# Sliding windows on one core: mixing stores of 4 KB runs and of 8 KB runs throughout

## Chip, cores and metric

One core of a Trainium2 chip. The metric is device time of one execution in microseconds (us); a median of several runs is given. Before: 196.94 us.

## The reference

The input is 16 images of 64 channels, 64 x 64, float32 (16.8 MB). Every 8 x 8 window at stride 4 is copied out, 15 x 15 windows per image (59.0 MB). There is no arithmetic.

```python
for i in range(n_h):
    for j in range(n_w):
        result[:, i, j] = x[:, :, 4*i : 4*i + 8, 4*j : 4*j + 8]
```

## The kernel before

The whole input is loaded into `L`. A partition holds an image, half of the channels (`ch`) and a quarter of the rows. `window(j, s, half)` builds on DVE (the vector engine), in the ring buffer `G`, the windows of column `j` and row slot `s` of all partitions, and GpSimd (POOL) issues one indirect store. A store of all 32 channels of a partition writes 128 runs of 8 KB; one of half of them writes 128 runs of 4 KB. In the last slot one partition in four has no window, and its index is out of bounds.

```python
UNITS = 18                                   # ring of 18 half-size buffers
G = gpool.tile([P, UNITS * HCL, WS, WS], f32, name="G")

def window(j, s, half):                      # half: 0, 1, or None for all channels
    ...                                      # next buffer g in the ring
    if not last:
        nc.vector.tensor_copy(out=g, in_=L[:, cs, s * ST : s * ST + WS, cols])
    else:                                    # lower rows come from the next partition
        nc.vector.tensor_copy(out=g[:, :, 0:ST, :], in_=L[:, cs, s * ST : RB, cols])
        nc.vector.stream_shuffle(out=g[:, :, ST:WS, :], in_=L[:, cs, 0:ST, cols], mask=nxt)
    ...
    st = nc.gpsimd.indirect_dma_start(out=o, out_offset=..., in_=g..., ...)

order = [(j, s) for j in range(NW) for s in range(NSLOT)]   # 60 windows
EARLY = 12
for half in range(2):
    for j, s in order[:EARLY]:
        window(j, s, half)                   # 24 stores of 4 KB runs
for j, s in order[EARLY:]:
    window(j, s, None)                       # 48 stores of 8 KB runs
```

The first halves of the early windows need only half of the loads, so they go out while the rest is loaded. After that the kernel is a stream of stores.

Of the kernel before, what the change touches and what calls it, by code (L numbers as in the profile page):

```python
# [1 line left out]

# [4 lines left out]


@with_exitstack  # L10
def kernel(
    ctx: ExitStack,
    tc: tile.TileContext,
    x: bass.AP,
    window_size: int,
    stride: int,
    out: bass.AP,
):
    nc = tc.nc
    P = nc.NUM_PARTITIONS  # L20

    B, C, H, W = x.shape
    Bo, NH, NW, Co, WSo, WSo2 = out.shape
    WS = int(window_size)
    ST = int(stride)
    assert Bo == B and Co == C and WSo == WS and WSo2 == WS

    f32 = mybir.dt.float32
    i32 = mybir.dt.int32
    ALU = mybir.AluOpType  # L30
    HQ = 4
    CH = P // (B * HQ)
    CL = C // CH
    RB = H // HQ
    NSLOT = RB // ST
    NWIN = NH * NW
    CFREE = CL * WS * WS
    assert HQ == 4 and CH == 2 and WS == 2 * ST

    lpool = ctx.enter_context(tc.tile_pool(name="lpool", bufs=1))  # L40
    ipool = ctx.enter_context(tc.tile_pool(name="ipool", bufs=1))
    gpool = ctx.enter_context(tc.tile_pool(name="gpool", bufs=1))


    L = lpool.tile([P, CL, RB, W], f32)
    x_v = x.rearrange("b (ch cl) (hq r) w -> hq (b ch) cl (r w)", ch=CH, hq=HQ)
    NCH = 4
    cw = CL // NCH
    for k in range(NCH):
        for q in range(HQ):  # L50
            (nc.sync, nc.scalar)[q % 2].dma_start(
                out=L[q::HQ, k * cw : (k + 1) * cw, :, :],
                in_=x_v[q, :, k * cw : (k + 1) * cw, :],
            )


    def itile(name):
        return ipool.tile([P, 1], i32, name=name)

    pi, tb, tq, tc_, idx, idx_last = (itile(n) for n in ("pi", "tb", "tq", "tc", "idx", "idx_last"))  # L60
    nc.gpsimd.iota(pi[:, :], pattern=[[0, 1]], base=0, channel_multiplier=1)  # L61
    nc.vector.tensor_scalar(out=tb[:, :], in0=pi[:, :], scalar1=3, scalar2=None, op0=ALU.logical_shift_right)  # L62
    nc.vector.tensor_scalar(out=tc_[:, :], in0=pi[:, :], scalar1=2, scalar2=1, op0=ALU.logical_shift_right, op1=ALU.bitwise_and)  # L63
    nc.vector.tensor_scalar(out=tq[:, :], in0=pi[:, :], scalar1=HQ - 1, scalar2=None, op0=ALU.bitwise_and)  # L64
    nc.vector.tensor_scalar(out=tb[:, :], in0=tb[:, :], scalar1=float(NWIN * CH), scalar2=None, op0=ALU.mult)  # L65
    nc.vector.tensor_tensor(out=tb[:, :], in0=tb[:, :], in1=tc_[:, :], op=ALU.add)  # L66
    nc.vector.tensor_scalar(out=tc_[:, :], in0=tq[:, :], scalar1=float(NSLOT * NW * CH), scalar2=None, op0=ALU.mult)  # L67
    nc.vector.tensor_tensor(out=idx[:, :], in0=tb[:, :], in1=tc_[:, :], op=ALU.add)  # L68

    nc.vector.tensor_scalar(out=tq[:, :], in0=tq[:, :], scalar1=float(HQ - 1), scalar2=float(2 * B * NWIN * CH), op0=ALU.is_equal, op1=ALU.mult)  # L70
    nc.vector.tensor_tensor(out=idx_last[:, :], in0=idx[:, :], in1=tq[:, :], op=ALU.add)  # L71


    HCL = CL // 2
    idx_h, idx_hlast = itile("idx_h"), itile("idx_hlast")
    for d, e in ((idx_h, idx), (idx_hlast, idx_last)):
        nc.vector.tensor_scalar(out=d[:, :], in0=e[:, :], scalar1=2.0, scalar2=None, op0=ALU.mult)  # L77
    o_v = out.rearrange("b i j (ch cl) r w -> (b i j ch) (cl r w)", ch=CH)
    o_h = out.rearrange("b i j (ch cl) r w -> (b i j ch) (cl r w)", ch=2 * CH)
    nxt = [min(p + 1, 31) for p in range(32)]  # L80


    UNITS = 18
    G = gpool.tile([P, UNITS * HCL, WS, WS], f32, name="G")
    at = 0

    def window(j, s, half):
        nonlocal at
        cols = slice(j * ST, j * ST + WS)
        last = s == NSLOT - 1  # L90
        if half is None:
            n, c0 = 2, 0
            at += at % 2
        else:
            n, c0 = 1, half * HCL
        u = at % UNITS
        at += n
        cs = slice(c0, c0 + n * HCL)
        g = G[:, u * HCL : (u + n) * HCL, :, :]
        if not last:  # L100
            nc.vector.tensor_copy(out=g, in_=L[:, cs, s * ST : s * ST + WS, cols])  # L101
        else:
            nc.vector.tensor_copy(out=g[:, :, 0:ST, :], in_=L[:, cs, s * ST : RB, cols])  # L103
            nc.vector.stream_shuffle(out=g[:, :, ST:WS, :], in_=L[:, cs, 0:ST, cols], mask=nxt)  # L104
        if half is None:
            o, ix = o_v, (idx_last if last else idx)
        else:
            o, ix = o_h, (idx_hlast if last else idx_h)
        st = nc.gpsimd.indirect_dma_start(  # L109
            out=o,  # L110
            out_offset=bass.IndirectOffsetOnAxis(ap=ix[:, 0:1], axis=0),
            in_=g.rearrange("p c r w -> p (c r w)"),
            in_offset=None,
            element_offset=(s * NW + j) * CH * CFREE + (half or 0) * HCL * WS * WS,
            bounds_check=B * NWIN * CH * (1 if half is None else 2) - 1,
            oob_is_err=False,
        )
        tc.declare_no_dep(st.ins, group="stores", reason="each store writes rows of its own")
        tc.add_to_no_dep_group("stores", st.ins)

    order = [(j, s) for j in range(NW) for s in range(NSLOT)]
    EARLY = 12
    for half in range(2):
        for j, s in order[:EARLY]:
            window(j, s, half)
    for j, s in order[EARLY:]:
        window(j, s, None)


# [1 line left out]
_INS = ['x', 'window_size', 'stride']  # L131
_OUTS = [((16, 15, 15, 64, 8, 8), 'float32')]

_NUMBERS = {'window_size': 8, 'stride': 4}


# [26 lines left out]
```

## Time and profile before

| | before |
|---|---|
| time, profiled span | 196.94 us, 194.9 us |
| DVE, POOL busy | 85.7 us (44%), 91.1 us (47%) |
| DMA: packets, bytes, mean | 14,723; 75.8 MB; 389 GB/s |
| stores | 72 |

Read this as a transfer problem. The DMA row of the page is at 9 nearly everywhere, and both engines are half idle.

### The profile page before, as it was taken

How to read it: one execution, taken by the hardware profiler on the slowest of the kernel's cores; microseconds unless marked ns; L12 is line 12 of the kernel's file. 1: busy time of each engine (PE TensorE's matmuls, PEld its weight loads, DVE VectorE, ACT ScalarE, POOL GpSimd, SP SyncE). 2: the span in 40 equal slices, each digit the busy share in tenths (PEclk: the TensorE clock that was granted, in tenths of full speed). 3: DMA queues.
4: the chain of work that ended last, by engine and by line, in shares of the span. 5: the costliest groups of instructions: out<-in, count | busy, mean ns of one | idle time of the engine just before them, and what ended most of it. 6: DMA issues, size and time to landing. Idle time of an engine off the chain costs nothing.

```text
span 194.9 us, 458 instructions
## 1 busy us (share of the span) xinstructions
DVE 85.7 (44%) x119; POOL 91.1 (47%) x77
## 2 busy tenths in 40 slices
DVE  2000069100699865464646464747474737430000
POOL 0000037723388888888854545454545454530000
DMA  5999999999999889999999999999999999999970
GB/s 182 419 401 415 409 409 414 423 420 419 419 415 421 353 334 387 403 414 398 403 409 405 414 405 407 410 403 412 407 414 407 412 409 409 409 407 419 422 298 20
DMA packets 14723, 75.79 MB, mean 389 GB/s; under 512 B 1984, under 2 KB 1984, under 8 KB 8960
## 3 DMA queue, kind: packets, MB, share of 16 engines
q0 software_dynamic: 10368, 58.99, 74.7%
q1 hardware_dynamic: 2176, 8.39, 10.9%
q10 hardware_dynamic: 2176, 8.39, 10.6%
q14 instruction: 3, 0.02, 0.0%
HBM read 16.78 MB, written 62.91 MB: 409 GB/s over the span
## 4 chain that ended last, share of the span: by engine, by line
DMA 52%; issue 28%; POOL 8%; POOLq 1%; PEldq 0%
DMA out_dram<-G,idx_last 38%; DMA out_dram<-G,idx_hlast 15%; POOL out_dram L109 8%; POOLq L158 1%; POOLq L109 0%; POOL pi L61 0%; PEldq L158 0%
## 5 line engine op out<-in xcount | busy, mean ns | idle before, releaser
L101 DVE COPY G<-L 128x2048 f32<-128x2048 f32 (+1 forms) x54 | 55.8, 1055 | 69.5 <-DMA L<-in_x_dram 39.5
L109 POOL DMA_INDIRECT out_dram<-G,idx x36 | 44.8, 1244 | 31.8 <-DMA out_dram<-G,idx 27.4
L109 POOL DMA_INDIRECT out_dram<-G,idx_h x18 | 22.5, 1250 | 37.8 <-DVE G L101 28.8
L109 POOL DMA_INDIRECT out_dram<-G,idx_last x12 | 16.7, 1392 | 8.9 <-DVE G L104 7.7
L104 DVE STREAM_SHUFFLE G<-L 128x1024 f32<-128x1024 f32 (+1 forms) x18 | 19.6, 1088 | 0.0
L103 DVE COPY G<-L 128x1024 f32<-128x1024 f32 (+1 forms) x18 | 11.6, 643 | 16.0 <-DMA out_dram<-G,idx 14.4
L109 POOL DMA_INDIRECT out_dram<-G,idx_hlast x6 | 6.8, 1130 | 3.7 <-DMA out_dram<-G,idx_hlast 2.5
L62 DVE TENSOR_SCALAR tb<-pi 128x1 int32<-128x1 int32 x1 | 0.2, 154 | 1.0 <-POOL pi L61 1.0
L61 POOL IOTA pi<- 128x1 int32 x1 | 0.1, 119 | 0.4 <-PEq L158 0.4
L104 DVE LOAD_MASK_SELECT G<-L x18 | 0.2, 12 | 0.0
L144 POOL MEMSET const-float32-0.0<- 128x1 f32 x1 | 0.1, 98 | 0.2 <-issue 0.2
L68 DVE CUSTOM_DVE_ANT_0 idx<-tb,tc 128x2 uint16<-128x2 uint16 x1 | 0.2, 160 | 0.0
L66 DVE CUSTOM_DVE_ANT_0 tb<-tb,tc 128x2 uint16<-128x2 uint16 x1 | 0.2, 159 | 0.0
L67 DVE TENSOR_SCALAR tc<-tq 128x1 int32<-128x1 int32 x1 | 0.2, 154 | 0.0
L77 DVE TENSOR_SCALAR idx_hlast<-idx_last 128x1 int32<-128x1 int32 x1 | 0.2, 154 | 0.0
L77 DVE TENSOR_SCALAR idx_h<-idx 128x1 int32<-128x1 int32 x1 | 0.2, 154 | 0.0
L71 DVE CUSTOM_DVE_ANT_0 idx_last<-idx,tq 128x2 uint16<-128x2 uint16 x1 | 0.2, 153 | 0.0
L65 DVE TENSOR_SCALAR tb<-tb 128x1 int32<-128x1 int32 x1 | 0.1, 149 | 0.0
L70 DVE TENSOR_SCALAR tq<-tq 128x1 int32<-128x1 int32 x1 | 0.1, 148 | 0.0
L63 DVE TENSOR_SCALAR tc<-pi 128x1 int32<-128x1 int32 x1 | 0.1, 145 | 0.0
L64 DVE TENSOR_SCALAR tq<-pi 128x1 int32<-128x1 int32 x1 | 0.1, 144 | 0.0
L144 POOL MEMSET const-uint8-127<- 128x1 uint8 x1 | 0.1, 118 | 0.0
(2 smaller groups left out, 0.2 us busy)
## 6 DMA issues: line engine op xcount, KB each, us to landing
L<-in_x_dram SPq DMA_DIRECT2D x8, 1024.0 KB, 19.9
L<-in_x_dram ACTq DMA_DIRECT2D x8, 1024.0 KB, 21.3
out_dram<-G,idx POOLq DMA_INDIRECT x36, 18.7
out_dram<-G,idx_h POOLq DMA_INDIRECT x18, 8.7
out_dram<-G,idx_last POOLq DMA_INDIRECT x12, 18.5
out_dram<-G,idx_hlast POOLq DMA_INDIRECT x6, 8.9
```

The costliest lines, as they stand in the source:

```text
L62: nc.vector.tensor_scalar(out=tb[:, :], in0=pi[:, :], scalar1=3, scalar2=None, op0=ALU.logical_shift_right)
L66: nc.vector.tensor_tensor(out=tb[:, :], in0=tb[:, :], in1=tc_[:, :], op=ALU.add)
L67: nc.vector.tensor_scalar(out=tc_[:, :], in0=tq[:, :], scalar1=float(NSLOT * NW * CH), scalar2=None, op0=ALU.mult)
L68: nc.vector.tensor_tensor(out=idx[:, :], in0=tb[:, :], in1=tc_[:, :], op=ALU.add)
L71: nc.vector.tensor_tensor(out=idx_last[:, :], in0=idx[:, :], in1=tq[:, :], op=ALU.add)
L77: nc.vector.tensor_scalar(out=d[:, :], in0=e[:, :], scalar1=2.0, scalar2=None, op0=ALU.mult)
L101: nc.vector.tensor_copy(out=g, in_=L[:, cs, s * ST : s * ST + WS, cols])
L103: nc.vector.tensor_copy(out=g[:, :, 0:ST, :], in_=L[:, cs, s * ST : RB, cols])
L104: nc.vector.stream_shuffle(out=g[:, :, ST:WS, :], in_=L[:, cs, 0:ST, cols], mask=nxt)
L109: st = nc.gpsimd.indirect_dma_start(out=o, out_offset=bass.IndirectOffsetOnAxis(ap=ix[:, 0:1], axis=0), in_=g.rearrange("p c r w -> p (c r ...
L144: nc = _bacc.Bacc("TRN2", target_bir_lowering=False, num_devices=1)
L158: with _tile.TileContext(nc) as tc:
```

## The change

The intent is to alternate short and long stores: the short ones drain faster than POOL issues them, and the long ones give it time. In the mixed part the second halves of the early windows alternate with full stores; afterwards one window in three is split in halves, so that the mixture goes on to the end.

```diff
-    for half in range(2):
-        for j, s in order[:EARLY]:
-            window(j, s, half)
-    for j, s in order[EARLY:]:
-        window(j, s, None)
+    for j, s in order[:EARLY]:
+        window(j, s, 0)
+    late = list(order[:EARLY])
+    rest = list(order[EARLY:])
+    while late:
+        for w in late[:2]:
+            window(*w, 1)
+        for w in rest[:2]:
+            window(*w, None)
+        late, rest = late[2:], rest[2:]
+    while rest:
+        window(*rest[0], 0)
+        window(*rest[0], 1)
+        for w in rest[1:3]:
+            window(*w, None)
+        rest = rest[3:]
```

There are 84 stores for 72. Twelve full stores became 24 half stores.

## The prediction

> **What bounds the kernel now.** I began with the page's busy strip. DVE (44% of the span) and POOL (47%) are half idle, and the DMA row is at 9 from the second slice to the 38th. The kernel moves 16.8 MB in and 59.0 MB out, so the question is how fast the sixteen DMA engines drain, and where they do not. I asked for the stages separately (columns: stretch, its length, DVE and POOL busy us with instruction counts, clock, DMA share, GB/s):
>
> ```profile
> 51.00:66.00 15.00, 15.00 (x26) 12.02 (x9) 1.00 1.03 418
> 66.00:73.00 7.00, 4.28 (x5) 5.78 (x5) 1.00 0.78 315
> 73.00:101.00 28.00, 15.04 (x15) 22.41 (x18) 1.00 1.00 403
> 101.00:171.00 70.00, 39.63 (x43) 36.22 (x29) 1.00 1.01 408
> 171.00:188.00 17.00, 1.28 (x3) 1.92 (x2) 1.00 0.99 407
> 188.00:195.00 7.00, 0.00 (x0) 0.00 (x0) 1.00 0.18 77
> ```
>
> The DMA engines are full from 51 to 66 us, where the second halves of the first twelve windows go out as 4 KB runs. They are short of work in one place, 66 to 73 us (0.78), and slightly below full while the 8 KB stores run. The last row is the drain of the slower engines and the closing sequence.
>
> Why 66 to 73 starves is in the timeline (start, length, engine, what, and in brackets the idle time before it):
>
> ```profile
> 59.30 3.48 DVE L101 COPY G<-L 128x2048 f32<-128x2048 f32 x3
> 60.93 1.97 POOL L109 DMA_INDIRECT out_dram<-G,idx_h  x1 [0.30 <-issue]
> ...
> 63.20 1.01 POOL L109 DMA_INDIRECT out_dram<-G,idx_hlast  x1 [0.30 <-DMA out_dram<-G,idx_hlast]
> ...
> 64.48 2.41 DVE L101 COPY G<-L 128x2048 f32<-128x2048 f32 x2
> 64.52 2.50 POOL L109 DMA_INDIRECT out_dram<-G,idx_h  x1 [0.30 <-DMA out_dram<-G,idx_h]
> 67.32 0.96 POOL L109 DMA_INDIRECT out_dram<-G,idx_h  x1 [0.31 <-issue]
> ```
>
> What to see: each POOL instruction issues one store. During DVE copies it lasts 1.97 or 2.50 us; alone it lasts 0.96. The twelve half stores after 51 us start at 51.54 to 70.48, one per 1.72 us (18.94/11), but a half store drains in about 1.27 us (below). POOL loses 0.45 us per store, uses up the backlog left from the loads, and at 67 us the engines run dry.
>
> Then POOL's waits (total us, times, longest) and the DMA issues (last number: median us from issue to landing):
>
> ```profile
> POOL out_dram L109 <- DMA out_dram<-G,idx: 27.7, 24, 1.6
> out_dram<-G,idx POOLq DMA_INDIRECT x36, 18.7
> out_dram<-G,idx_h POOLq DMA_INDIRECT x18, 8.7
> ```
>
> An 8 KB store lands 18.7 us after its issue, about 7 stores of work at one per 2.44 us (four windows, one with 96 rows, per 9.77 us). The landing records use eight semaphores in turn, so POOL waits for the store eight back: the queue is limited to eight stores, whatever their size. In the late stage it is always deep; DVE and POOL only have to keep it from emptying.
>
> Finally I read the single landings and packets in the trace. Each store gives 16 landings, one per DMA engine, in two groups of eight. For the store landing at about 77 us the first and last engine are 0.16 us apart, at 161 us 3.4 us, at the end 3.5 us. So eight slower engines set the end: they take about 2.60 us per 8 KB store, the others 2.50. During 4 KB stores the spread stays at 0.8 to 1.0 us and does not grow. Packet times agree: 4 KB is 159 ns nearly always; 8 KB is 309 at best and 322 on average (338 while POOL issues beside a shuffle, 315 when neither works). The last data land at 191.2; closing takes 3.7 us, and the measured time is 2.0 above the span.
>
> **What the Trainium skill says.** "DMA: Bandwidth & Descriptors", section "Where 436 GB/s comes from", puts the ceiling of 16 engines at 435 GB/s. By that, 4 KB on one engine is 151 ns and 8 KB 301 ns (my estimate from the page); the trace's minima, 159 and 309, are each 8 ns more, so they agree with a ceiling and a small cost per packet. The same page, "Why small descriptors are slow (HBM only)", says that each packet has a fixed overhead of about 3 cycles; the trace shows such an overhead, about 8 ns. "SBUF — State Buffer", section "SBUF: two separate sides", says that DVE's fp32 SBUF-to-SBUF copy locks GpSimd out while it runs, so that it can't write DMA descriptors. The trace agrees: the POOL instruction of 2.50 us lies beside 2.41 us of copies.
>
> **The change part by part.** The first twelve half stores and their loads stay as they are; nothing moves before 51 us. Of the following, 12 of 48 full windows become 24 half windows (9 complete pairs and 3 last-slot pairs), interleaved with the twelve second halves so that two halves alternate with two fulls to the end. There are 84 stores for 72.
>
> 1. *The dip, removed.* On the slow engines, the landings from 68.0 to 76.9 us cover three halves, one last half and one full: 3×1.28 + 0.97 + 2.55 = 7.36 us of work in 8.9, so 1.5 us were idle, and another 0.1 at the next store: 1.6 us. After the change POOL issues 3 MB per four stores, which drains in 2×1.27 + 2×2.55 = 7.6 us; at its bad pace of 1.72 us POOL needs 6.9. The backlog at 51 us is seven half stores, to 58.7 us, so the first full stores are behind work already queued. DVE can fill about 11 free half-size buffers and then waits for landings, which also releases POOL. I see no dip: −1.6 us.
>
> 2. *More packets, added.* Splitting an 8 KB run costs 2×159 − 309 = 9 ns, for eight runs per engine 72 ns, plus one 9 ns completion packet: 0.08 us per full window. The last-slot windows count as 0.75, so 11.25 × 0.08 = +0.9 us over undisturbed 8 KB packets.
>
> 3. *Slow packets, moved.* On the slow engines a full store takes 2.60, not 2.48 (8×309 + 9 ns), and two halves 2.56. If 4 KB packets are really immune, those windows get shorter: 11.25 × (2.56 − 2.60) = −0.45, in place of +0.9. If instead the loss belongs to each POOL issue (about 0.09 us, 3.4 us over 38 stores), the 12 extra issues meet 8 KB packets two thirds of the time, and the full stores lose more: the +0.9 stays and up to +0.3 joins it. I take the middle, +0.4.
>
> 4. *Instructions.* Twelve copies of 1.24 us turn into 24 of about 0.67: +1.2 us on DVE (shuffles similar: 0.71 for half of 1.28). POOL has 12 more issues of 1.0 to 1.4 us: about +15. Both lie beside the DMA; DVE has idle gaps of 1.4 us at every late wait. Path: 0.
>
> Sum: −1.6 + 0.4 = −1.2, so 196.9 becomes 195.7 us.
>
> **Rivals.** *The shallower queue starves.* Eight mixed stores are 6 MB, not 8. At 2.5 us per MB that is 15 us. Fast engines 3.5 us ahead still have over 8 us queued when the eighth store back lands, and a new issue takes under 2 us. I don't expect it; if the alternation made POOL late anyway, I would see DMA share near 0.95 and 199 to 203 us. *POOL becomes the bound.* 84 issues with 1.7 to 2.5 us beside copies: if the mean were over 1.9 us per store, as in 59 to 67 us now, the dip would spread over the mixed stage. Against it: copies take only half of DVE's time once buffers are full (issues then last 0.96 to 1.39 now). It would give 198 to 201. *The dip is hidden anyway:* the fast engines wait 2.3 us there and the slow ones catch up by the difference, so the spread starts again at 0.16. Without the dip the existing 0.9 us spread is kept and grows. I counted slow engines alone for this reason; if they have some slack I missed, the gain is nil and steps 2 and 3 leave 197 to 198. *Best case:* immunity of the 4 KB packets holds, −2.05: 194.9.
>
> **Range and chances.** The certain parts are the dip (0 to −1.6) and packets (−0.45 to +1.2), which span 194.9 to 198.1 us; the extremes together are unlikely, so 194.5 to 197.7 with a little room below for 4 KB traffic that keeps the engines level. Faster by 2% means under 193.0, which needs a gain that I find in no row; slower by 2% means over 200.9, only by starvation. Chances 0.03, 0.92, 0.05.
>
> **What would show it.** Step 1: the DMA share between 60 and 80 us at 1.0 or more, no landing latency under 7 us there. Step 2: packets of 4 KB at 159 ns in the mixed stage too. Step 3: the spread between first and last engine; if it ends under 3 us the immunity holds, if over 4 us the loss follows the issues. Step 4: DVE about 87 us busy, POOL 100 to 110. I am wrong if the 4 KB packets get slower than 165 ns when mixed, or if DMA share falls below 1.0 in the late stage.

## The result, and the profile after

The changed kernel takes 196.81 us (196.75 to 196.88) for 196.94: a ratio of 0.9994, 95% interval 0.9977 to 1.0012. Ratios are the mean time of one kernel's fast runs over that of the other's of the same rounds, so not quite the ratio of the medians. I had forecast 195.7, a gain of 1.2 us; there is none to be seen.

The stages of the changed kernel (stretch, length, DVE and POOL busy with counts, clock, DMA share, GB/s):

```profile
51.00:66.00 15.00, 13.75 (x20) 12.32 (x9) 1.00 1.02 420
66.00:73.00 7.00, 5.20 (x7) 5.47 (x6) 1.00 1.02 422
73.00:101.00 28.00, 16.83 (x26) 22.15 (x18) 1.00 1.02 412
101.00:171.00 70.00, 40.45 (x56) 43.10 (x38) 1.00 1.02 403
171.00:188.00 17.00, 0.47 (x1) 4.09 (x5) 1.00 0.93 373
```

The gap from 66 to 73 us is gone: 422 GB/s for 315. From 73 to 101 it is faster too, 412 for 403. Then it loses: 403 for 408 over 70 us, at full DMA share, with 38 stores issued for 29. The DMA engines are as busy as before and move less: each packet takes longer. The last stretch, 373 for 407, is no sign of loss by itself, as part of the engines are done earlier there; e1 below, which is faster, has 369.

The timeline of the changed kernel where the gap was:

```profile
60.19 2.00 POOL L109 DMA_INDIRECT out_dram<-G,idx_hlast  x1 [0.30 <-issue]
62.49 1.02 POOL L109 DMA_INDIRECT out_dram<-G,idx  x1 [0.30 <-issue]
...
63.81 1.77 POOL L109 DMA_INDIRECT out_dram<-G,idx_last  x1 [0.30 <-DVE G L104]
65.89 0.98 POOL L109 DMA_INDIRECT out_dram<-G,idx_h  x1 [0.30 <-issue]
```

POOL is as slow beside copies as before (2.00, 1.77), but two of these stores are long, and the DMA engines live on them. Its waits, and the time from issue to landing:

```profile
POOL out_dram L109 <- DMA out_dram<-G,idx: 21.1, 18, 1.7
out_dram<-G,idx POOLq DMA_INDIRECT x27, 13.9
out_dram<-G,idx_h POOLq DMA_INDIRECT x36, 13.6
```

A full store lands 13.9 us after its issue, not 18.7: the queue is eight stores deep as before, but they hold less. It never runs dry.

The single landings in the trace give the account. "Late eight" are the eight landings of each store, of sixteen, that come last. "Closing" is the time from the last landing to the end of GpSimd's final drain.

| | before | after |
|---|---|---|
| first to last engine, last store | 3.5 us | 5.4 us |
| last landing | 191.17 us | 190.85 us |
| closing | 2.99 us | 3.48 us |
| mean of a 4 KB packet, late stage (90 to 130 us) | none there | 166.8 ns |
| 8 KB packet, same stretch | 324 ns | 324 ns |

So 0.3 us was gained at the last landing, and 0.5 us lost in the closing.

### The profile page after: what moved, and what is told of

The parts are those of the page before. It is cut to its first block, busy times and chain, and to the rows that moved or that the text cites. A ratio compares the mean times of both kernels' runs of the same rounds, so it can differ in the third digit from the quotient of the medians.

```text
span 195.1 us, 526 instructions
## 1 busy us (share of the span) xinstructions
DVE 87.4 (45%) x137; POOL 99.9 (51%) x89
## 4 chain that ended last, share of the span: by engine, by line
DMA 70%; issue 19%; POOL 1%; POOLq 1%; PEldq 0%
DMA out_dram<-G,idx 27%; DMA out_dram<-G,idx_last 21%; DMA out_dram<-G,idx_h 18%; DMA out_dram<-G,idx_hlast 4%; POOL out_dram L109 1%; POOLq L169 1%; POOLq L109 0%; POOL pi L61 0%; PEldq L169 0%
## 5 line engine op out<-in xcount | busy, mean ns | idle before, releaser
L101 DVE COPY G<-L 128x1024 f32<-128x1024 f32 (+1 forms) x63 | 57.4, 936 | 69.2 <-DMA L<-in_x_dram 39.1
L109 POOL DMA_INDIRECT out_dram<-G,idx_h x36 | 40.5, 1124 | 43.0 <-DVE G L101 26.0
L109 POOL DMA_INDIRECT out_dram<-G,idx x27 | 32.5, 1205 | 20.0 <-DMA out_dram<-G,idx 12.4
L104 DVE STREAM_SHUFFLE G<-L 128x512 f32<-128x512 f32 (+1 forms) x21 | 20.0, 953 | 0.0
L103 DVE COPY G<-L 128x512 f32<-128x512 f32 (+1 forms) x21 | 11.8, 564 | 13.7 <-DMA out_dram<-G,idx 12.2
L109 POOL DMA_INDIRECT out_dram<-G,idx_hlast x12 | 15.0, 1247 | 5.9 <-issue 3.4
L109 POOL DMA_INDIRECT out_dram<-G,idx_last x9 | 11.6, 1288 | 9.2 <-DMA out_dram<-G,idx 8.3
## 6 DMA issues: line engine op xcount, KB each, us to landing
out_dram<-G,idx POOLq DMA_INDIRECT x27, 13.9
```

Source lines behind the costliest of these rows:

```text
L109: st = nc.gpsimd.indirect_dma_start(out=o, out_offset=bass.IndirectOffsetOnAxis(ap=ix[:, 0:1], axis=0), in_=g.rearrange("p c r w -> p (c r ...
```

## The experiments

Each edit is against the kernel before or the one named. Main theory after the result: the gap was worth what I had said, and the twelve extra stores take it back, by longer packets and by a longer closing. Rival: the gap had been slack of the late engines, and the split is nearly free. Two theories of the longer packets are set against each other: the issue theory (each store that GpSimd issues disturbs the packets in flight) and the 4 KB theory (4 KB packets among 8 KB ones are slow). "Disturbed" means longer than the minimum of 159 or 309 ns.

### e1_dip_only: the first part alone

```diff
 (changed kernel)
-    while rest:
-        window(*rest[0], 0)
-        window(*rest[0], 1)
-        for w in rest[1:3]:
-            window(*w, None)
-        rest = rest[3:]
+    for w in rest:
+        window(*w, None)
```

> Only the first part of the change: the second halves of the twelve early windows alternate with full stores, all later windows stay full; 72 stores as before. Main theory: the dip was worth about 1.6 us on the engines that end last and the change lost it again elsewhere, by slower packets on those engines and by a longer closing (3.0 us from last landing to the end of GpSimd's final drain with 72 stores, 3.5 us with 84, so about 0.041 us per store). Then this run takes 195.3 us (195.0 to 195.7), its closing drain ends 3.0 us after the last landing, and no slice between 60 and 80 us is under 400 GB/s. Rival: the idle time of the dip was slack of the late engines, which the skew uses up anyway; then 196.6 to 197.0.

Measured: 194.77 us, ratio 0.9888 (0.9870 to 0.9905). The rival falls: without the gap the kernel gains 2.1 us. The closing is 2.99 us. Its stages:

```profile
51.00:66.00 15.00, 13.97 (x21) 12.22 (x8) 1.00 1.02 421
66.00:73.00 7.00, 5.38 (x7) 5.67 (x5) 1.00 1.02 424
73.00:101.00 28.00, 16.46 (x21) 22.82 (x18) 1.00 1.02 414
101.00:171.00 70.00, 39.50 (x43) 37.15 (x31) 1.00 1.01 409
```

Up to 101 us it is the changed kernel; from there it keeps 409 GB/s with 31 stores. The gain is larger than the 1.6 us expected. By the last landings, about 1.6 us less is lost up to 75 us, as predicted, and another 0.6 from 75 to 100, where before's packets are already disturbed. Packets of e1 are undisturbed (309 and 159 ns) until 78 us; in the kernel before, those of 8 KB are longer from 75 us, right after the gap.

### e2_split_only: the second part alone

```diff
-    for j, s in order[EARLY:]:
-        window(j, s, None)
+    rest = list(order[EARLY:])
+    for g in range(0, len(rest), 4):
+        cut = rest[g + (g // 4) % 4]
+        window(*cut, 0)
+        window(*cut, 1)
+        for w in rest[g : g + 4]:
+            if w != cut:
+                window(*w, None)
```

> Only the second part: the early windows as before, with the dip, and twelve of the 48 later windows split in two halves, 84 stores as in the changed kernel. Main theory: 0.5 us of closing, about 0.3 of packet overhead and 0.5 to 0.9 of slower packets on the late eight engines: 198.0 to 198.5 us. Rival (the dip is slack and the split is nearly free): 196.8 to 197.4.

Measured: 200.14 us, ratio 1.0162 (1.0146 to 1.0177), closing 3.48 us. Worse than both, and by more than expected. Part of it is a longer gap:

```profile
66.00:73.00 7.00, 4.60 (x5) 5.75 (x5) 1.00 0.74 298
73.00:101.00 28.00, 16.21 (x23) 22.51 (x19) 1.00 0.98 389
```

After the gap the queue is shallow, and the half stores put in there keep it so (0.98, 389). The parts are therefore not additive: split stores cost more behind a gap (+3.3 us) than in a full queue (+2.1 us, changed kernel against e1).

### e3_empty24 and e6_empty24_tied: stores that move nothing

Twenty-four stores with every index out of bounds are added to e1: 24 issues and no bytes.

```diff
+    def empty(g):      # e3: source L, no dependence; e6: source g, the buffer just stored
+        nc.gpsimd.indirect_dma_start(out=o_v, out_offset=<idx_none>, in_=g, ...)
     for k, w in enumerate(rest):
         g = window(*w, None)
+        if k < 36 and k % 3 != 2:        # e3: without k < 36
+            empty(g)
```

> The dip-free kernel (e1) with 24 more stores whose rows are all out of bounds: 96 issues, no further byte, no 4 KB packet beyond those of e1. If the closing grows with the number of stores, the final drain ends 96 x 0.041 = 3.9 to 4.0 us after the last landing, 1.0 more than in e1. If the slower packets come from the number of issues of GpSimd, the late eight engines take 2.70 us or more per full store and the time is e1 + 3 us; if they come from the 4 KB packets themselves, the late eight stay at 2.61 and the time is e1 + 1.2 us (1.0 closing, 0.2 for 24 x 9 tiny packets).

Measured: 211.32 us, ratio 1.0729. This run failed as a test of packets: the empty stores depended on nothing, so 19 of the 24 were issued early, nine in the load phase and ten in a row from 54 to 69 us, where they starved the queue (DMA share 0.45 from 55 to 76 us). It settles the closing: 3.97 us for 96 stores, as expected. It also shows an empty store alone landing 2.06 to 2.10 us after its issue. "DMA: Bandwidth & Descriptors", section "Anatomy of one DMA — SWDGE (gpsimd) path", of the Trainium skill gives about 2.0 us of fixed time, and agrees.

The mended version:

> As e1, with 24 stores of nothing among the late full stores, each tied to the buffer of the full store before it, so that they are issued there and not early as in e3. Issue theory: 24 x 0.14 = 3.4 us on the late engines, 24 x 0.041 = 1.0 of closing, up to 0.3 of tiny packets: 199.1 to 199.5 us, late eight engines lose about 0.14 us per issue. Theory of 4 KB packets: 194.8 + 1.3 = 196.1 us.

Measured: 198.38 us, ratio 1.0072 (1.0055 to 1.0089). That is 3.6 us over e1 (1.0072 - 0.9888 = 0.0184, times 196.9), 0.15 us per store; the 4 KB theory had 1.3, the issue theory 4.3 to 4.7. Closing 3.97 us, so 1.0 of the 3.6. Another 1.0 us or so would be the tiny packets themselves, nine per engine and store (an estimate: such packets follow one another at 4 to 6 ns in this trace). That leaves about 1.6 us, 0.07 per issue. Part of that is starving:

```profile
101.00:171.00 70.00, 39.07 (x43) 56.76 (x43) 1.00 0.99 387
```

The share is 0.99, and the first and last engine of the last store are only 0.9 us apart, for 4.6 in e1: the faster engines had to wait. So e6 alone does not settle what an issue costs.

### e5_row_split: 84 stores, no further 4 KB packets

```diff
 (changed kernel)
-        window(*rest[0], 0)
-        window(*rest[0], 1)
+        window(*rest[0], None, split=True)   # one copy, two stores of 8 KB runs, each with
+                                             # the other half of the rows out of bounds
```

> As the changed kernel, 84 stores in the same order, but the twelve later windows are split by rows, not by channels: each of the two stores moves the 8 KB runs of half of the partitions, and the other half of its indices is out of bounds. No 4 KB packet is added to those of e1. In the traces so far the late eight engines lose 0.135 to 0.144 us beyond undisturbed packets per store issued after about 77 us, whatever its size (before 1.8 us for 13 stores in 30 us, e1 1.7 for 13, changed kernel 2.3 for 17). If the loss belongs to the issue, this run takes e1 + 12 x 0.14 + 0.5 of closing + 0.1 of tiny packets = 194.8 + 2.3 = 197.1 us (196.4 to 197.7). If it belongs to 4 KB packets among 8 KB ones, e1 + 0.6 = 195.4 us.

Measured: 197.15 us, ratio 1.0008 (0.9993 to 1.0023): the issue theory had 197.1, the 4 KB theory 195.4. The late stage is that of the changed kernel (403), and it has the same 38 stores:

```profile
101.00:171.00 70.00, 38.74 (x43) 46.98 (x38) 1.00 1.02 402
```

For the last 36 windows, which are identical work, the late eight take 87.35 us in e1, 89.32 in the changed kernel and 89.45 here. So the 4 KB packets are not what costs. The rows out of bounds do add 108 tiny packets per engine to those of e1 (page: 3,712 under 512 B for 1,984), about 0.5 us by the same estimate; that leaves 1.6 us, as in the changed kernel. The disturbance can be counted: between 100 and 172 us, packets exceed their undisturbed length by the following sums (per DMA engine, mean of all sixteen).

| | stores issued | excess, us | per store |
|---|---|---|---|
| before | 30 | 3.05 | 0.102 |
| e1 | 31 | 3.02 | 0.097 |
| changed | 39 | 3.59 | 0.092 |
| e5 | 39 | 3.71 | 0.095 |
| e6 | 44 | 3.53 | 0.080 |

At equal numbers of issues it is nearly the same for 4 KB and 8 KB packets (changed, e5), and it grows with the number, but less than in proportion: 0.57 us for eight issues from e1 to the changed kernel, nothing more from there to e6. In e4 below it is only 2.2 us for 52 issues, 0.042 each. So no fixed price per issue follows from this table. The late eight carry more of it than the others.

### e9_no_copy_late: DVE taken away

```diff
 (e1)
-        if not last:
+        if not copy:                  # the last 36 windows; wrong result on purpose
+            pass
+        elif not last:
```

> As e1, but the last 36 windows are stored without being copied: the stores send what lies in the buffers, so the result is wrong on purpose. DVE is idle after about 85 us, the stores and their issues are those of e1. If the disturbance of the late eight engines (about 1.7 us per 30 us) comes from GpSimd's issues alone, it stays: 194.3 to 195.2 us, late eight at 2.60 us per full store. If it needs DVE's copies or shuffles, full stores take 2.46 to 2.52 us on all engines and the time is 191.5 to 193.0 us.

Measured: 194.35 us, ratio 0.9868 (0.9853 to 0.9883).

```profile
101.00:171.00 70.00, 0.00 (x0) 27.91 (x29) 1.00 1.01 410
```

With DVE at 0.00 the rate is 410 for 409, and the excess is 2.96 us for 29 stores, 0.102 each. Full stores take 2.59 us on the late eight. 8 KB packets that lie within an issue are about 21 ns longer than undisturbed, those outside 6 ns (e1: 21 and 6). DVE is not the cause of the late disturbance. Is it the issue, or the landing that releases it? Counted from the last landing of a store, the lengthening is greatest at 0.4 to 0.6 us in e9 (32 ns) and at 1.4 to 1.6 us in e1 (35 ns), where DVE's copy holds the issue up. Counted back from the end of an issue, it is greatest 0.6 to 0.8 us before in both (30 and 28 ns). So it moves with the issue, not with the landing. In the changed kernel, e5 and e6, where issues are denser, 8 KB packets are as long outside of issues as inside (16 or 17 ns over, by their midpoints), so there this test says nothing; 4 KB packets are 10 ns over inside and 7 outside in the changed kernel, 7 and 2 in e4.

### e4_all_half: every window split

```diff
-    for j, s in order[EARLY:]:
-        window(j, s, None)
+    for w in order[EARLY:]:
+        window(*w, 0)
+        window(*w, 1)
```

> Every window in two halves: 120 stores of 4 KB runs. Main theory: closing 5.0 us; GpSimd needs about 1.7 us per store beside DVE's copies but a half store drains in 1.25 to 1.36, so the engines starve throughout, as in the dip: 205 to 215 us with DMA share about 0.85 after 70 us. Rival: GpSimd keeps up because DVE's copies take only half of the time once the buffers are full: 200 us or less, and then a 4 KB packet's mean in the late stage shows whether 4 KB alone is immune (159 to 161 ns) or not (165 to 168).

Measured: 214.79 us, ratio 1.0924. POOL is the bound, as the main theory had it:

```profile
101.00:171.00 70.00, 39.67 (x75) 54.76 (x51) 1.00 0.91 357
```

51 stores in 70 us, 1.37 us each: POOL is busy or in the 0.3 us between two issues all the time. 4 KB packets take 165.0 ns from 90 to 130 us, so they are not immune even alone. The closing is 0.62 us, not 5.0: a miss that I can't explain. In the late stage only two or three earlier stores are still under way when POOL issues the next; before, e1 and the changed kernel have six or seven.

### e7_early12_empty and e11_early4_empty: is the start of the disturbance counted in issues?

In the changed kernel and in e1 packets are undisturbed until 77 to 78 us, just when POOL issues its 29th store. Empty stores in the load phase move that count.

```diff
 (e1)
+    for _ in range(12):      # e11: 4
+        empty()
```

> As e1, with 12 stores of nothing issued before 27 us, while GpSimd waits for the loads. In e1 and in the changed kernel packets are undisturbed (309 and 159 ns) until 77 to 78 us, when GpSimd issues its 29th store, and disturbed by about 0.14 us per issue afterwards. If the start of the trouble is counted in issues[...], it moves to the 17th real store, at about 59 us, and 12 more issues are disturbed: e1 + 1.7 + 0.5 of closing = 197.0 us. If it is a matter of time or of depth, it stays at 77 us: e1 + 0.6 = 195.4 us.

> As e1 with four stores of nothing in the load phase: 76 issues, few enough that the first halves are issued as before. By the price per issue: 4 x 0.041 of closing plus, if the disturbance starts with the 29th issue (then at about 72 us, not 77 to 78), 4 x 0.12: 195.4 us. If the start is a matter of time: 195.0 us and still 77 to 78.

e7: 200.72 us, ratio 1.0190. Inconclusive: the empty stores held up the early halves, so that a gap opened (DMA share 0.85 from 50 to 60 us) and the disturbance began there, at 54. e11 is clean: 194.53 us, ratio 0.9876 (0.9861 to 0.9891), within e1's interval. The 29th issue is at 73 us, but the disturbance still starts at 78. It isn't counted in issues. The closing grew by 0.16 us, as four stores should; the total does not show it, within its interval.

### e8_early8, e10_early10 and e12_full_first: can e1 be beaten?

```diff
 (e1)
-    EARLY = 12
+    EARLY = 8           # e8, with two full stores before two second halves; e10: 10
```

```diff
 (e1)                    # e12: the order in the mixed part
-        for w in late[:2]:
-            window(*w, 1)
         for w in rest[:2]:
             window(*w, None)
+        for w in late[:2]:
+            window(*w, 1)
```

> A version meant to beat both: eight early windows in halves, not twelve, so 68 stores; two full stores come before each two second halves, and all later windows are full. Four issues fewer than e1: 4 x (0.14 + 0.041) + 4 x 0.03 of packet overhead = 0.85 us: 193.9 us, if the backlog at 50 us, now three half stores, is enough. If it is not, a new gap of 1 to 2 us in the DMA share at 50 to 56 us and 195 to 196.

> As e1 with ten early windows in halves, not twelve: 70 stores. By the price found so far (0.15 to 0.20 us per issue, of which 0.041 is closing) two issues fewer give 194.8 - 0.35 = 194.4 us (194.1 to 194.7), if the backlog of five half stores at 50 us is enough; it lasts until about 56 us and the first new store is issued at 51.7. If it is not enough: a gap in the DMA share at 55 us and 195.5 or more, as with eight (e8). Also: if undisturbed packets end with the 29th issue, the disturbance starts at 81 us or later, not at 77 to 78.

> As e1, 72 stores, but in the mixed stage two full stores come before two second halves, so the backlog after 51 us grows (two stores of 2.5 us each before two of 1.25) where in e1 it stays near 7.5 us. In e10, with a smaller backlog, packets became disturbed at 64 us, in e1 at 78. If a deeper backlog holds the disturbance off, it starts after 80 us here and the time is 194.3 to 194.6 us; if its start has nothing to do with the backlog, it stays at 77 to 78 us and the time at 194.7 to 194.9. A third outcome, an earlier start, would speak against any order by backlog.

e8: 197.36 us, ratio 1.0019. The backlog of three half stores was too small, DMA share 0.31 from 52 to 54 us. e10: 195.16 us, ratio 0.9914 (0.9900 to 0.9927). Two issues fewer, yet about 0.4 us slower than e1 (the intervals just overlap): the disturbance starts at 64 us, and the DMA share falls to 0.95 from 68 to 70 us. e12: 194.65 us, ratio 0.9886 (0.9869 to 0.9902), equal to e1; the deeper backlog doesn't delay the start beyond 78 us. So e1 stands: 1.1% faster than either kernel, clear of noise, but small.

## Why the prediction was wrong

**Step 1, the dip, held.** It is gone, the DMA share is 1.02 from 66 to 73 us, and no landing takes less than 7 us there. Removing it alone gives 2.1 us (e1). The 1.6 us of idle time were sized right; that packets stay undisturbed for longer without the gap, worth about 0.5 to 0.6, I had not seen. (The busy strip, which I read as 9 throughout, shows 88 at the gap.)

**Step 2, more packets, was too large.** Undisturbed 4 KB packets start 155 ns apart and 8 KB packets 306: the recorded lengths overlap a little. So each takes 4 or 5 ns more than the 151 and 301 estimated above, not 8, and a split costs 4 ns, not 9. Between 66 and 75 us of the changed kernel and e1 a half store takes 1.242 us and a full one 2.456, so a window in halves costs 2 x 1.242 - 2.456 = 0.03 us more, not 0.08: 0.3 us in all, not 0.9.

**Step 3, slow packets, failed, and it decided the result.** I allowed for 4 KB packets being immune, because they took 159 ns in the gap's neighbourhood, and took "the middle, +0.4" for steps 2 and 3. They are not immune: until about 77 us packets of both sizes are at their minimum in the changed kernel and e1, and later 4 KB packets take 166.8 ns, over the 165 that the prediction had named as the sign of being wrong. The other branch of that step, "the loss belongs to each POOL issue", was the right one, but I sized it at up to +0.3 by counting only issues that meet 8 KB packets. That sum was wrong in itself: two thirds of twelve issues at 0.09 us are 0.7. Measured against e1, the last landing is 1.9 us later (190.85 for 188.96): 0.3 of packets, and 1.6 that remain and are put down to the disturbance by twelve issues. (The part counted directly is 0.57 us, on the mean of all engines and from 100 to 172 us alone.) The prediction's test by the final spread, "over 4 us", came out at 5.4, but it does not separate the two: e1, with no more stores, ends at 4.6. And the trace before already pointed at POOL, where I had blamed POOL beside a shuffle: from 73 us on, 8 KB packets take 329 ns by their midpoints with POOL alone at work, 316 with DVE alone and 316 with neither.

**Step 4, instructions, left out a term.** DVE's and POOL's busy times came as said (87.4 and 99.9 us), but "Path: 0" is false for the twelve issues. GpSimd's final drain ends 0.0415 us per store after the last landing: 2.82 us with 68 stores, 2.99 with 72, 3.48 with 84, 3.97 with 96. That is +0.5 us at the very end.

The sum with measured terms: -2.1 (e1) + 0.3 + 1.6 (the remainder) + 0.5 = +0.3, for a span that grew by 0.2 and a time that is unchanged within 0.2%. That last digit lies within the scatter between profiled spans.

**The rivals.** Neither did the queue starve, although it is shallower, nor was POOL the bound (its mean is 1.19 us per issue). "The dip is hidden anyway" forecast the time of 197 nearly right for a wrong reason: e1 shows that it wasn't hidden.

**What stays open.** What starts the disturbance. With a backlog kept up, it starts at 77 to 79 us in seven kernels, whatever the count of issues (e11) or the order (e12), although POOL issues just as densely before; after a gap, at once; with a small backlog, at 64 us (e10). e9 says nothing of the start, as DVE still copies until 82 us there. Nor do the runs show how an issue lengthens packets, why e4's issues cost so little, or why eight engines suffer more.

## What to carry to other kernels

When DMA engines are full, count the stores as well as the bytes. Here each extra indirect store cost 0.15 to 0.20 us on the path (2.1 us for the twelve of the change, 2.4 for e5's, with its tiny packets, 3.6 for e6's 24), although the engine that issues it was half idle. So split a transfer only where the queue would otherwise run dry, and run the two parts of a change alone before you take a sum of nil to mean that neither did anything.

## What the Trainium skill lacked or had wrong

- No page has the closing: GpSimd's final drain ends 0.0415 us per indirect store after the last landing (68 to 96 stores; the exception is e4, 0.62 us for 120).
- No page has that packets in flight are longer while GpSimd issues a store: from 100 us on, 8 KB packets within an issue are about 21 ns over the undisturbed 309, outside 6 ns (e9, DVE idle). Before 77 us the issues of the same run did not lengthen them. "SBUF — State Buffer", section "SBUF: two separate sides", has only the other direction, descriptors that DVE's copies hold up; that one is borne out (2.00 us for 0.96).
- "DMA: Bandwidth & Descriptors", section "Latency and other measured facts", says that DMA engines 7 and 15 are usually slower than the others. Here eight of the sixteen are, by 3.5 us at the end of the kernel before and 5.4 us in the changed one; the trace doesn't name them. The page's guess at a cause, contention at the ports of the descriptor rings, is not tested by any run.
- The same page, section "Why small descriptors are slow (HBM only)", speaks of about 3 cycles per packet and gives no time for it. The runs show 4 ns for one more packet in a full stream (2 x 155 - 306), where recorded lengths had suggested 9.
